# Neighbourhood attention at the two edge blocks of the grid: 384 keys per query tile in place of 512

## The chip, the cores and the metric

The kernel runs on one core of one Trainium2 chip. The metric is the device time of one launch in microseconds. A core has five engines with a queue of instructions each: TensorE (PE in the profile; its weight loads have a row of their own, PEld), VectorE (DVE), ScalarE (ACT), GpSimd (POOL) and SyncE (SP), which here issues every DMA.

## The reference, cut to what matters

One encoder layer over 2048 tokens of width 1024. A combined projection gives six pieces; the first two go through a state-space model (S5), the other four through neighbourhood attention on a grid of 32 rows by 64 columns, and both results are projected out and mixed with the residual. The part that the change touches:

```python
def neighborhood_attention_2d(q, k, v, rpb):
    rows = seqlen // GRID_W            # 32 rows of 64 tokens
    kh = min(NA_ROWS_MAX, rows)        # 8
    row_start = jnp.clip(r - kh // 2, 0, rows - kh)
    col_start = jnp.clip(c - NA_COLS // 2, 0, GRID_W - NA_COLS)   # 16 columns
    ...
    scores = jnp.einsum('brqhd,brikhd->bhrqik', q, k_blk) * scale + bias
    scores = jnp.where(col_in[:, None, :], scores, jnp.finfo(f32).min)
    probs = jax.nn.softmax(scores, axis=(-2, -1))
    out = jnp.einsum('bhrqik,brikhd->brqhd', probs, v_blk)
```

Each of 8 heads of 64 dimensions lets a query see 8 rows by 16 columns of neighbours. The window is clamped at the grid's borders, so queries of the uppermost 8 rows reach no key below row 10, and queries of the lowest 8 rows none above row 20.

## The kernel before, in words

The kernel has three stages: a projection and state-space stage (to about 650 us of the span), attention beside other matmuls (about 655 to 1056 us), and a dense last stage (to 1387 us).

**Units and steps.** Attention runs over 16 units. A unit is one pair of heads (`hp`, the pair lies in partitions 0 to 63 and 64 to 127) and one block `i` of 8 grid rows. The first eight units are blocks 1 and 2, the last eight are the edge blocks 3 and 0 (`na_units`, L681). A unit has four steps, one for each query tile `j` of 8 rows by 16 columns, 128 queries; so there are 64 steps, and steps 32 to 63 belong to edge blocks. For every tile the keys are a frame of 16 rows by 32 columns, 512 keys, that starts 4 rows above the block. In an edge block four of these rows lie outside the grid; there the frame holds rows of the other edge, and the bias (-1e30) masks them.

**One step**, for each head of the pair:
- `scores` (L718): a matmul of 64 rows by 128 columns of weights with 512 moving columns into PSUM tile `p_qk` (L726; two tiles, one for each head, in all). DVE adds the bias and takes the row minimum (L730), ACT takes the exponential and its sum (L732), DVE the reciprocal (L733), POOL the product (L734).
- `turn` (L738): four transposes of 128 by 128 into `p_pt` (L744), one ACT copy to SBUF (L746).
- `weigh` (L749): the product with v for one group `jk` of key columns that two query tiles share: two matmuls a head of 256 moving columns (L757), for the lower and upper half of the 16 rows. The two heads' matmuls write partitions 0 to 63 and 64 to 127 of the PSUM tile `po`.

All operands are fp32; of each L726 and L757 matmul the trace has two records (two passes), of each transpose one.

**What sets the order.** `attention` (L760) writes two steps a round: turn, scores, products of two earlier steps, turn, scores, and then `fill`, a counted number of matmuls of other work (`beside`, L872): the last projections, the GLU (L662), and from about 876 us on the output projection of eight mix tiles (`mix_tile`, L855, matmuls L834). PE's order is fixed by the program (`issue_after`). The orders of the other queues, SP's too, and of the instructions inside one `scores` call are made by the framework's scheduler from its own model of time.

**Loads.** Each unit's bias (L697), q (L699), k (L702), v (L703) and gate zn (L705) come by DMA from DRAM into rings of two buffers, and a load waits until the unit before last has let its buffer go. The result of a unit goes out at L713 (`yn_scr`); a mix tile loads it back at L860, casts it on ACT (L863, `yh`), takes the rest on DVE (L864, `yl`), and its two PSUM banks are copied out by ACT (L868) and DVE (L869). Three banks serve these tiles, so the second matmul of a tile waits for a copy of the tile before.

Of the kernel before, what the change touches and what calls it, by code (L numbers as in the profile page):

```python
# [50 lines left out]
class Layer:  # L51
# [633 lines left out]
    def na_units(self):  # L685
# [4 lines left out]
        for blocks in ((1, 2), (3, 0)):  # L690
            for hp in range(4):
                kind = None
                for n, i in enumerate(blocks):
                    it = (0, 1, 1, 2)[i]
                    if it != kind:
                        bm, kind = self.b_bm(), it
                        nc.sync.dma_start(bm, a["bias"][hp, it])  # L697
                    q, k, v, zn = self.b_q(), self.b_k(), self.b_v(), self.b_zn()
                    nc.sync.dma_start(q, self.q_scr[hp][:, 512 * i : 512 * i + 512])  # L699
                    for lo, rows in ((0, slice(i - 1, i + 1)),) if i else ((0, slice(3, 4)), (1, slice(0, 1))):  # L700
                        c = slice(512 * rows.start, 512 * rows.stop)
# [13 lines left out]

                    yield js, q, k, v, bm, done

    def scores(self, j, q, k, bm):  # L718

        nc, c = self.nc, self.const  # L720
        ps, out = [self.ps2("qk") for _ in range(2)], []
        for par in range(2):
            own = slice(64 * par, 64 * par + 64)
            kk = k[own]
            mv = ap_of(kk, max(16 * (j - 1), 0), [list(kk.ap[0]), [48 if j == 0 else 16, 2], [64, 16], [1, 16]])
            nc.tensor.matmul(ps[par], q[own, 128 * j : 128 * j + 128], mv, start=True, stop=True)  # L726
        for par in range(2):
            s = self.b_s()
# [9 lines left out]
    def turn(self, j, ss, pts):  # L738

        nc = self.nc  # L740
        for s, pT in zip(ss, pts):
            pt = self.ps2("pt")
            for n in range(4):
                nc.tensor.transpose(pt[:, 128 * n : 128 * n + 128], s[:, 128 * n : 128 * n + 128], self.ident)  # L744
            base, step = ((j - 1) * 512 + 128, 512 if j == 3 else 384) if j else (0, 1536)
            nc.scalar.copy(ap_of(pT, base, [list(pT.ap[0]), [step, 2], [256, 2], [1, 128]]),  # L746
                           pt.rearrange("p (j i q) -> p j i q", j=2, i=2))

    def weigh(self, po, jk, v, pts, first, last):  # L749

        for rb in range(2):
            for par in range(2):
                own = slice(64 * par, 64 * par + 64)
                pw = po[own]
                o = ap_of(pw, 128 * jk % 384, [list(pw.ap[0]), [384 if jk == 3 else 128, 2], [1, 128]])
                c = 512 * jk + 256 * rb
                self.nc.tensor.matmul(o, v[:, 4 * rb + jk, own], pts[par][:, c : c + 256],  # L757
                                      start=first and rb == 0, stop=last and rb == 1, skip_group_check=True)

    def attention(self, fill):  # L760
# [9 lines left out]
        def turn(t):  # L770
            if 0 <= t < STEPS:
                _, j, ss, pp = st[t]
                run(self.turn, j, ss, pp)

        def score(t):
            if t < STEPS:
# [4 lines left out]
                with self.tc.issue_after(self.last_pe()):  # L781
                    st[t] = (u, j, self.scores(j, u[1], u[2], u[4]), pts)

        def product(t):
            if 0 <= t < STEPS:
                n = t % 4
                (_, _, _, v, _, done), j, _, pp = st.pop(t)
                if n == 0:
                    self.po = self.ps.tile([128, 512], F32, tag="pv", name="po", bufs=1)
                else:  # L790
                    run(self.weigh, self.po, (j - 1) % 4, v, pp, n == 1, False)
                if n == 3:
                    run(self.weigh, self.po, j, v, pp, False, True)
                    done(self.po)
# [195 lines left out]
def biases(rpb):  # L990
# [3 lines left out]
    for it, i in enumerate((0, 1, 3)):  # L994
        for jt, j in enumerate((0, 1, 3)):
            qr, qc = (8 * i + np.arange(128) // 16)[:, None], (16 * j + np.arange(128) % 16)[:, None]
            r0, c0 = np.clip(qr - 4, 0, 24), np.clip(qc - 8, 0, 48)
            n = np.arange(512)
            half, rr, cc = n // 256, n // 16 % 16, n % 16
            kr = (8 * i - 4 + rr)[None, :]  # L1000
# [49 lines left out]
```

## Time and profile before

| what | value |
|---|---|
| median of 3 runs | 1385.05 us (1382.8 to 1385.6) |
| the profiled execution | 1388.96 us, span of its trace 1387.2 us |
| PE busy over the span | 1319.9 us (95%) |
| DVE, ACT, POOL busy | 895.0 us (65%), 461.0 us (33%), 560.2 us (40%) |
| edge blocks, 841 to 1056 us | PE busy 201.9 of 215 us, clock 0.88 to 1.00 |

Busy time is the union of an engine's instructions. Matmuls are pipelined: a record lasts longer than the distance to the next one, so the time that PE needs for a row of matmuls is read from where the next group starts. The granted clock is TensorE's, 1.00 being 2.4 GHz and 0.50 being 1.2 GHz.

### The profile page before, as it was taken

The numbers are of one execution on the slowest core, as the hardware profiler recorded it, in microseconds if no ns is written. First come the engines' busy times: TensorE is split into PE (matmuls) and PEld (weight loads), VectorE is DVE, ScalarE is ACT, GpSimd is POOL, SyncE is SP. The second block draws the span as 40 slices with busy tenths as digits, with TensorE's granted clock in tenths as the row PEclk, the third lists the DMA queues.
The fourth block names the chain that finished last, engine by engine and source line by source line (L and its number), as shares of the span: only waits on it lengthen the run. The fifth ranks groups of instructions, "written<-read, shape, count | busy, mean of one in ns | idle before, by whom it ended". The sixth has DMA issues, their size and how long they took to land. (4 is left out here: it accounts for less than half of the span.)

```text
span 1387.2 us, 19010 instructions
## 1 busy us (share of the span) xinstructions
PE 1319.9 (95%) x6432; PEld 1026.2 (74%) x6432; DVE 895.0 (65%) x1851; ACT 461.0 (33%) x957; POOL 560.2 (40%) x695
## 2 busy tenths in 40 slices
PE   7897999999999999999996898999999999999998
PEld 6675778888878888887664676666667888888887
DVE  5864899888977779533456566533343344888886
ACT  7520211111111122112555565644443322333322
POOL 5968789677766665000333444222220000121121
PEclk9998999999999999999998999999999999999999
DMA  8873223223333332226357567746425532333331
GB/s 280 247 204 84 75 86 100 86 85 97 91 82 80 84 82 90 80 74 217 114 173 258 185 216 241 254 161 226 152 77 193 179 106 83 100 121 119 106 123 63
DMA packets 177665, 190.01 MB, mean 137 GB/s; under 512 B 46496, under 2 KB 136992, under 8 KB 175904
## 3 DMA queue, kind: packets, MB, share of 16 engines
q1 hardware_dynamic: 177568, 188.80, 43.3%
q8 instruction: 51, 0.84, 0.2%
q14 instruction: 46, 0.38, 0.1%
HBM read 131.44 MB, written 57.31 MB: 136 GB/s over the span
## 5 line engine op out<-in xcount | busy, mean ns | idle before, releaser
L205 PE MATMUL pd<-xh,wh 128*128 128x512 f32 x768 | 311.6, 407 | 19.5 <-DVE ev_u L267 12.4
L205 PE MATMUL pd<-xl,wh 128*128 128x512 f32 x768 | 308.2, 402 | 0.0
L205 PE MATMUL pd<-xh,wl 128*128 128x512 f32 x768 | 307.7, 401 | 0.0
L734 POOL TENSOR_SCALAR na<-na,rs 128x512 f32<-128x512 f32 x128 | 94.8, 744 | 365.4 <-DVE rs L733 304.2
L205 PEld LDWEIGHTS pd<-xh,wh 128*128 128x128 f32 x768 | 146.0, 190 | 57.8 <-DVE ev_u L267 13.5
L205 PEld LDWEIGHTS pd<-xh,wl 128*128 128x128 f32 x768 | 145.7, 190 | 38.7 <-issue 4.0
L205 PEld LDWEIGHTS pd<-xl,wh 128*128 128x128 f32 x768 | 145.9, 190 | 35.7 <-issue 1.5
L730 DVE CUSTOM_DVE_ANT_0 na<-p_qk,na 128x512 f32<-128x512 f32 x128 | 83.8, 687 | 115.9 <-PE p_qk L726 112.1
L977 POOL TENSOR_TENSOR p3e<-p3e,p 128x1024 f32<-128x1024 f32 x15 | 39.2, 2611 | 292.7 <-DVE p3e L972 284.9
L834 PE MATMUL pd<-wo,yh 128*128 128x512 f32 x512 | 142.5, 394 | 7.3 <-ACT o L868 4.1
L834 PE MATMUL pd<-wg,yh 128*128 128x512 f32 x512 | 140.7, 391 | 0.0
L834 PEld LDWEIGHTS pd<-wo,yh 128*128 128x128 f32 x512 | 96.0, 189 | 34.7 <-ACT o L868 5.4
L732 ACT ACTIVATE na<-na,mn 128x512 f32<-128x512 f32 x128 | 91.7, 717 | 66.9 <-DVE mn L730 66.5
L834 PEld LDWEIGHTS pd<-wg,yh 128*128 128x128 f32 x512 | 95.5, 188 | 19.2
L746 ACT COPY na<-p_pt 128x512 f32<-128x512 f32 x128 | 68.8, 583 | 76.3 <-PE p_pt L744 76.3
L178 ACT ACTIVATE wh<-wr 128x512 fp32r<-128x512 f32 x48 | 28.1, 624 | 164.1 <-PE pd L205 146.8
L834 PE MATMUL pd<-wo,yl 128*128 128x512 f32 x256 | 81.8, 394 | 0.0
L834 PE MATMUL pd<-wg,yl 128*128 128x512 f32 x256 | 81.3, 391 | 0.0
L744 PE MATMUL p_pt<-ident,na 128*128 128x128 f32 x512 | 70.9, 282 | 8.7 <-POOL na L734 6.4
L726 PE MATMUL p_qk<-na,na 64*128 64x512 f32 x256 | 76.5, 653 | 2.5 <-DVE mn L730 2.5
L744 PEld LDWEIGHTS p_pt<-ident,na 128*128 128x128 f32 x512 | 58.6, 144 | 25.1 <-issue 13.7
L757 PE MATMUL po<-na,na 128*64 128x256 f32 x512 | 63.2, 390 | 0.0
(203 smaller groups left out, 2256.5 us busy)
## 6 DMA issues: line engine op xcount, KB each, us to landing
na<-in_bias_dram SPq DMA_DIRECT2D x12, 1536.0 KB
wr<-in_w_in_dram SPq DMA_DIRECT2D x48, 256.0 KB
xr<-in_xT_dram SPq DMA_DIRECT2D x32, 256.0 KB
xn<-in_x_dram SPq DMA_DIRECT2D x32, 256.0 KB
o_scr<-o SPq DMA_DIRECT2D x16, 512.0 KB
p<-o_scr SPq DMA_DIRECT2D x16, 512.0 KB
xt<-in_x_dram SPq DMA_DIRECT2D x16, 512.0 KB
out_dram<-p3e SPq DMA_DIRECT2D x15, 512.0 KB
```

The source lines that it names most:

```text
L178: nc.scalar.mul(wh[:, sl], wr, mul)
L205: nc.tensor.matmul(ps, st[:, k, :], mv[:, k, :], start=n == 0, stop=n == 3 * KT - 1)
L726: nc.tensor.matmul(ps[par], q[own, 128 * j : 128 * j + 128], mv, start=True, stop=True)
L730: nc.vector.tensor_tensor_reduce(out=s, in0=ps[par], in1=bm[:, par, (0, 1, 1, 2)[j]], scale=-1.0, scalar=3e38, op0=ALU.add, op1=ALU.min, a ...
L732: nc.scalar.activation(s, s, AF.Exp, bias=mn, scale=-1.0, accum_out=sm)
L734: nc.gpsimd.tensor_scalar(s, s, rs, 1.0, ALU.mult, ALU.mult)
L744: nc.tensor.transpose(pt[:, 128 * n : 128 * n + 128], s[:, 128 * n : 128 * n + 128], self.ident)
L746: nc.scalar.copy(ap_of(pT, base, [list(pT.ap[0]), [step, 2], [256, 2], [1, 128]]), pt.rearrange("p (j i q) -> p j i q", j=2, i=2))
L757: self.nc.tensor.matmul(o, v[:, 4 * rb + jk, own], pts[par][:, c : c + 256], start=first and rb == 0, stop=last and rb == 1, skip_group_ch ...
L834: nc.tensor.matmul(ps[e], st[:, k, :], mv[k][:, 512 * e : 512 * e + 512], start=k == 0 and n == 0, stop=k == nk - 1 and n == 2)
L977: nc.gpsimd.tensor_add(th, th, h1)
```

## The change

For the eight units of blocks 3 and 0 the frame of keys is cut to the 12 rows that lie in the grid, 8 rows first (`kt` = 0 or 1 says which half of the frame they are) and then 4: 384 keys. Units of blocks 1 and 2 keep 512 (`kt` is None). The scores of a head become a matmul of 256 and one of 128 columns; the minimum, exponential and product run over 384 columns; three transposes in place of four; and the product with v becomes, for each `jk`, one matmul a head of 256 columns over the 8-row half (L779), and for each tile `j` one a head of 128 columns over the 4 rows (new `weigh_rest`, L786), for which 64 partitions hold rows of one column half and 64 of the other. The bias load brings 384 of 512 columns (still two heads by three tiles), so each partition's piece becomes six pieces. The v load of an edge unit becomes five DMAs (one of 256 KB, two of 96 KB, two of 32 KB) in place of one of 512 KB (block 3) or two of 256 KB (block 0). For all units the transposed probabilities are stored in one row for each tile, and the product reads two stretches of 128 columns in place of one of 256.

```diff
@@ na_units
+                    kt = (1, None, None, 0)[i]
                     if it != kind:
                         bm, kind = self.b_bm(), it
-                        nc.sync.dma_start(bm, a["bias"][hp, it])
+                        nk = 512 if it == 1 else 384
+                        nc.sync.dma_start(bm[:, :, :, 0:nk], a["bias"][hp, it][:, :, :, 0:nk])
...
-                        nc.sync.dma_start(v[:, 4 * lo : 4 * lo + 4 * (rows.stop - rows.start)],
-                                          self.v_scr[hp][rows].rearrange("i j p d -> p (i j) d"))
+                    if it == 1:
+                        nc.sync.dma_start(v, self.v_scr[hp][i - 1 : i + 1].rearrange("i j p d -> p (i j) d"))
+                    else:
+
+                        nc.sync.dma_start(v[:, 4 * kt : 4 * kt + 4], self.v_scr[hp][0 if i == 0 else 2].rearrange("j p d -> p j d"))
+                        vl = v[:, 4 - 4 * kt : 8 - 4 * kt]
+                        rest = self.v_scr[hp][3][:, 64 * kt : 64 * kt + 64].rearrange("j p d -> p j d")
+                        nc.sync.dma_start(vl[0:64, 1:4], rest[:, 0:3])
+                        nc.sync.dma_start(vl[64:128, 1:4], rest[:, 1:4])
+                        nc.sync.dma_start(vl[0:64, 0:1], rest[:, 0:1])
+                        nc.sync.dma_start(vl[64:128, 0:1], rest[:, 3:4])
@@ scores
+        n, rows = (512, ((0, 16),)) if kt is None else (384, ((8 * kt, 8), (8 - 4 * kt, 4)))
+        at = 0
+        for r0, nr in rows:
+            for par in range(2):
+                own = slice(64 * par, 64 * par + 64)
+                kk = k[own]
+                mv = ap_of(kk, max(16 * (j - 1), 0) + 64 * r0,
+                           [list(kk.ap[0]), [48 if j == 0 else 16, 2], [64, nr], [1, 16]])
+                nc.tensor.matmul(ps[par][:, at : at + 32 * nr], q[own, 128 * j : 128 * j + 128], mv, start=True, stop=True)
+            at += 32 * nr
...
-            nc.vector.tensor_tensor_reduce(out=s, in0=ps[par], in1=bm[:, par, (0, 1, 1, 2)[j]], scale=-1.0, scalar=3e38,
-                                           op0=ALU.add, op1=ALU.min, accum_out=mn)
+            nc.vector.tensor_tensor_reduce(out=s, in0=ps[par][:, 0:n], in1=bm[:, par, (0, 1, 1, 2)[j], 0:n], scale=-1.0,
+                                           scalar=3e38, op0=ALU.add, op1=ALU.min, accum_out=mn)
@@ turn
-            for n in range(4):
-                nc.tensor.transpose(pt[:, 128 * n : 128 * n + 128], s[:, 128 * n : 128 * n + 128], self.ident)
+            n = 512 if kt is None else 384
+            for x in range(0, n, 128):
+                nc.tensor.transpose(pt[:, x : x + 128], s[:, x : x + 128], self.ident)
+            nc.scalar.copy(pT[:, n * j : n * j + n], pt[:, 0:n])
@@ weigh
+        n, wide = (512, 2) if kt is None else (384, 1)
+        at = lambda q, h: n * q + 128 * wide * h
+        for rb in range(wide):
...
+    def weigh_rest(self, po, j, v, pts, kt):
+
+        for par in range(2):
+            own = slice(64 * par, 64 * par + 64)
+            self.nc.tensor.matmul(po[own, 128 * j : 128 * j + 128], v[:, 4 - 4 * kt + j, own],
+                                  pts[par][:, 384 * j + 256 : 384 * j + 384], start=False, stop=False, skip_group_check=True)
@@ attention, product
+                    if kt is not None:
+                        for jj in js[0 if n == 1 else n : n + 1]:
+                            run(self.weigh_rest, self.po, jj, v, pp, kt)
```

PE, one round in the edge blocks, before: transposes (`p_pt`), scores (`p_qk`), product with v (`po`), transposes, scores; the row's end says how many matmuls run one after another.

```order
L744 MATMUL p_pt<-ident,na_5624 128x128 x8
L726 MATMUL p_qk<-na_5623,na_5621 128x512 x2
L757 MATMUL po<-na_5626,na_5623 64x256 x4
L744 MATMUL p_pt<-ident,na_5624 128x128 x8
L726 MATMUL p_qk<-na_5623,na_5621 128x512 x2
```

The corresponding round of the changed kernel, after the same matmuls of the mix tile:

```order
L763 MATMUL p_pt<-ident,na_5624 128x128 x6
L742 MATMUL p_qk<-na_5623,na_5621 128x256 x2
L742 MATMUL p_qk<-na_5623,na_5621 128x128 x2
L779 MATMUL po<-na_5626,na_5623 64x256 x2
L786 MATMUL po<-na_5626,na_5623 64x128 x4
L763 MATMUL p_pt<-ident,na_5624 128x128 x6
L742 MATMUL p_qk<-na_5623,na_5621 128x256
L742 MATMUL p_qk<-na_5623,na_5621 128x128
L742 MATMUL p_qk<-na_5623,na_5621 128x256
L742 MATMUL p_qk<-na_5623,na_5621 128x128
```

Two transposes of eight are gone in each step, and the first scores stand as 256, 256, 128, 128 columns (heads 0, 1, 0, 1). In the second scores of the round the scheduler has put both matmuls of head 0 ahead of those of head 1. The fill between rounds has the same number of matmuls as before in every round.

SP's queue, before, where the loads of the second edge unit meet the first mix tile's load (`y<-yn_scr_122`):

```order
L671 DMA ys_scr_120<-zs 128x1024
L642 DMA zs<-zs_scr_95 128x1024
L703 DMA na_5623<-v_scr_87 128x8x128
L713 DMA yn_scr_122<-na_5622 128x512
L705 DMA na_5624<-zn_scr_94 128x512
L699 DMA na_5621<-q_scr_79 128x512
L702 DMA na_5623<-kk_scr_83 128x512
L697 DMA na_5622<-in_bias_dram 128x3072
L702 DMA na_5623<-kk_scr_83 128x512
L860 DMA y<-yn_scr_122 128x4x128
```

The same place after:

```order
L714 DMA na_5623<-v_scr_87 64x128
L709 DMA na_5623<-v_scr_87 128x4x128
L712 DMA na_5623<-v_scr_87 64x3x128
L724 DMA yn_scr_122<-na_5622 128x512
L713 DMA na_5623<-v_scr_87 64x3x128
L715 DMA na_5623<-v_scr_87 64x128
L716 DMA na_5624<-zn_scr_94 128x512
L701 DMA na_5621<-q_scr_79 128x512
L699 DMA na_5622<-in_bias_dram 128x6x384
L704 DMA na_5623<-kk_scr_83 128x512 x2
L892 DMA y<-yn_scr_122 128x4x128
L671 DMA ys_scr_120<-zs 128x1024
```

The store of `yn_scr_122` now stands behind three of the five pieces of v, and two further pieces, in all four more issues, stand ahead of the mix tile's load; the bias load has 384 of 512 columns.

## Rows read from the trace of the kernel before

**Rows 1.** The page, busy time of each engine over the span.

```profile
PE 1319.9 (95%) x6432; PEld 1026.2 (74%) x6432; DVE 895.0 (65%) x1851; ACT 461.0 (33%) x957; POOL 560.2 (40%) x695
```

**Rows 2.** Windows: stretch, length, busy time by engine, granted clock, DMA share, GB/s.

```profile
841.00:870.00 29.00, 25.32 (x152) 18.00 (x151) 16.59 (x37) 15.98 (x35) 12.27 (x13) 0.88 0.73 249
870.00:1041.00 171.00, 163.67 (x900) 110.00 (x899) 67.19 (x196) 84.89 (x188) 39.27 (x56) 1.00 0.51 172
1041.00:1056.00 15.00, 12.88 (x72) 9.87 (x72) 3.17 (x4) 4.81 (x8) 0.02 (x1) 0.89 0.41 133
1056.00:1387.00 331.00, 325.84 (x1505) 270.18 (x1501) 225.22 (x595) 99.04 (x208) 39.16 (x15) 1.00 0.36 119
```

**Rows 3.** PE's waits in 841-870, then 870-1041: us, times, longest.

```profile
PE pd L662 <- ACT th L667: 1.8, 1, 1.8
PE p_qk L726 <- DVE mn L730: 1.8, 2, 1.1
...
PE pd L834 <- ACT o L868: 4.1, 3, 1.4
PE pd L834 <- DVE o L869: 3.2, 3, 1.3
```

**Rows 4.** Timeline of PE: start, length, instructions, number of records; edge rounds.

```profile
942.40 1.03 PE L744 MATMUL p_pt<-ident,na 128*128 128x128 f32 x8
943.36 1.13 PE L726 MATMUL p_qk<-na,na 64*128 64x512 f32 x4
944.42 1.08 PE L757 MATMUL po<-na,na 128*64 128x256 f32 x8
...
956.39 2.81 PE L757 MATMUL po<-na,na 128*64 128x256 f32 x24
```

**Rows 5.** The same timeline cut at 943.6 us: scores begun by then.

```profile
943.36 0.70 PE L726 MATMUL p_qk<-na,na 64*128 64x512 f32 x2
```

**Rows 6.** Timeline of PE in the stage before: one matmul of 256 columns.

```profile
577.77 0.59 PE L568 MATMUL p_qk<-x,gt 128*128 128x256 f32 x2
```

**Rows 7.** Groups by line on PE, 841-1056 us: records, busy us, mean ns, idle.

```profile
L726 PE MATMUL p_qk<-na,na 64*128 64x512 f32 x128 | 38.0, 646 | 1.8 <-DVE mn L730 1.8
L744 PE MATMUL p_pt<-ident,na 128*128 128x128 f32 x268 | 36.8, 280 | 2.2 <-ACT na L746 2.1
L757 PE MATMUL po<-na,na 128*64 128x256 f32 x284 | 34.6, 385 | 0.0
```

**Rows 8.** Instructions of lines L730, L732, L667: ns min/median/max, first and last start.

```profile
L730 DVE CUSTOM_DVE_ANT_0 na<-p_qk,na x128: 672/687/693, 656.8 to 1036.9; 128x512 f32<-128x512 f32 x128
...
L732 ACT ACTIVATE na<-na,mn x128: 704/722/727, 657.5 to 1038.8; 128x512 f32<-128x512 f32 x128
...
L667 ACT ACTIVATE th<-pd,bgh x32: 451/460/478, 744.0 to 877.1; 128x256 f32<-128x256 f32 x32
```

**Rows 9.** Timeline of SP and ACT around the first mix tile's load.

```profile
834.21 0.37 SPq L703 DMA_DIRECT2D na<-v_scr  x1
834.93 0.33 SPq L713 DMA_DIRECT2D yn_scr<-na  x1
...
837.73 0.33 SPq L697 DMA_DIRECT2D na<-in_bias_dram  x1
...
841.22 0.57 SPq L860 DMA_DIRECT2D y<-yn_scr  x1
...
849.73 1.05 ACT L863 CAST yh<-y 128x1024 fp32r<-128x1024 f32 x1 [3.66 <-DMA y<-yn_scr]
```

**Rows 10.** Windows, columns as in group 2: the slow stretch behind these waits.

```profile
861.60:868.20 6.60, 6.60 (x27) 5.47 (x26) 4.12 (x12) 4.87 (x12) 2.71 (x4) 0.50 0.95 286
```

**Rows 11.** Timeline of SP: loads of a later edge unit.

```profile
909.99 0.93 SPq L703 DMA_DIRECT2D na<-v_scr  x2
...
913.94 0.33 SPq L697 DMA_DIRECT2D na<-in_bias_dram  x1
```

More of the change, by code (lines that the diff above doesn't have):

```diff
@@ L714, in done, with scores @@
                         self.attended += n
-                    yield js, q, k, v, bm, done
-    def scores(self, j, q, k, bm):
+                    yield js, q, k, v, bm, done, kt
+    def scores(self, j, q, k, bm, kt):
         nc, c = self.nc, self.const
         ps, out = [self.ps2("qk") for _ in range(2)], []
-        for par in range(2):
[L723 to L728, printed above, removed]
+        n, rows = (512, ((0, 16),)) if kt is None else (384, ((8 * kt, 8), (8 - 4 * kt, 4)))
[8 more added lines that the diff above has]
+            at += 32 * nr
+        for par in range(2):
+            s = self.b_s()[:, 0:n]
             mn, sm, rs = (c.tile([128, 1], F32, tag=t, name=t, bufs=8) for t in ("mn", "sm", "rs"))
-            nc.vector.tensor_tensor_reduce(out=s, in0=ps[par], in1=bm[:, par, (0, 1, 1, 2)[j]], scale=-1.0, scalar=3e38,
-                                           op0=ALU.add, op1=ALU.min, accum_out=mn)
+            nc.vector.tensor_tensor_reduce(out=s, in0=ps[par][:, 0:n], in1=bm[:, par, (0, 1, 1, 2)[j], 0:n], scale=-1.0,
+                                           scalar=3e38, op0=ALU.add, op1=ALU.min, accum_out=mn)
             nc.scalar.activation(s, s, AF.Exp, bias=mn, scale=-1.0, accum_out=sm)
@@ L742, in turn, with weigh @@
             pt = self.ps2("pt")
-            for n in range(4):
-                nc.tensor.transpose(pt[:, 128 * n : 128 * n + 128], s[:, 128 * n : 128 * n + 128], self.ident)
[L745 to L751, printed above, removed]
+            n = 512 if kt is None else 384
+            for x in range(0, n, 128):
+                nc.tensor.transpose(pt[:, x : x + 128], s[:, x : x + 128], self.ident)
+            nc.scalar.copy(pT[:, n * j : n * j + n], pt[:, 0:n])
+    def weigh(self, po, jk, v, pts, kt, first, last):
+        (qa, ha), (qb, hb) = ((0, 1), (3, 1)) if jk == 3 else ((jk, int(jk > 0)), (jk + 1, 0))
+        n, wide = (512, 2) if kt is None else (384, 1)
+        at = lambda q, h: n * q + 128 * wide * h
+        for rb in range(wide):
             for par in range(2):
@@ L754, in weigh @@
                 pw = po[own]
[L755 to L758, printed above, removed]
+                o = ap_of(pw, 128 * qa, [list(pw.ap[0]), [128 * (qb - qa), 2], [1, 128]])
+                pT = pts[par]
+                mv = ap_of(pT, at(qa, ha) + 128 * rb, [list(pT.ap[0]), [at(qb, hb) - at(qa, ha), 2], [1, 128]])
+                self.nc.tensor.matmul(o, v[:, 4 * (rb if kt is None else kt) + jk, own], mv,
+                                      start=first and rb == 0, stop=last and rb == wide - 1, skip_group_check=True)
+    def weigh_rest(self, po, j, v, pts, kt):
[3 more added lines that the diff above has]
+                                  pts[par][:, 384 * j + 256 : 384 * j + 384], start=False, stop=False, skip_group_check=True)
     def attention(self, fill):
@@ L771, in turn @@
             if 0 <= t < STEPS:
-                _, j, ss, pp = st[t]
-                run(self.turn, j, ss, pp)
+                u, j, ss, pp = st[t]
+                run(self.turn, j, ss, pp, u[6])
         def score(t):
@@ L781, in score @@
                 with self.tc.issue_after(self.last_pe()):
-                    st[t] = (u, j, self.scores(j, u[1], u[2], u[4]), pts)
+                    st[t] = (u, j, self.scores(j, u[1], u[2], u[4], u[6]), pts)
         def product(t):
@@ L997, in biases @@
             r0, c0 = np.clip(qr - 4, 0, 24), np.clip(qc - 8, 0, 48)
-            n = np.arange(512)
-            half, rr, cc = n // 256, n // 16 % 16, n % 16
+            r = np.concatenate([np.stack(np.meshgrid(np.arange(2), x, np.arange(16), indexing="ij"), -1).reshape(-1, 3)
+                                for x in ((np.arange(8, 16), np.arange(4, 8)), (np.arange(16),),
+                                          (np.arange(8), np.arange(8, 12)))[it]])
+            half, rr, cc = r.T
             kr = (8 * i - 4 + rr)[None, :]
```

8 lines of the change are left out of this document (4 added, 4 removed).

## The prediction

> **What bounds the kernel now.** I read the page first: PE is busy for 95% of the span [rows 1], no other engine for more than 65%. An average over stages says little, so the windows come next. In the edge blocks' stretch, 841 to 1056 us, PE is busy 25.3 + 163.7 + 12.9 of 215 us; in its long middle it is busy for 163.7 of 171 us at clock 1.00, while DVE has 67 and ACT 85 of the 171 us, and in the dense last stage PE has 325.8 of 331 us [rows 2]. What PE waits for there is short: 7.3 us in the middle, all of it for the copies of a mix tile's PSUM banks, and 3.6 us at the start of the stretch [rows 3]. PE's order and its fill are the same before and after, so PE time taken out of the edge steps moves everything behind it forward. The sum is therefore one of PE time; the other engines' savings count only where PE waits for them.
>
> **What PE pays for a column.** Durations don't tell, since records overlap; distances do. A product group of 24 records lasts 2.81 us and one of 8 lasts 1.08 [rows 4]: 16 more records, 1.73 us. The records run in pairs, as the scores show: two of them are under way by 943.6, together 0.70 us long, though one alone has a mean of 646 ns, and all four end after 1.13 us [rows 4, 5, 7]. A pair must be the two heads, since the two passes of one matmul use the same rows of weights. So 1.73 us are 8 pair-passes of 256 columns, 0.216 us each. A lone matmul of 256 columns, two records in 0.59 us with a last one of about 0.38, is paced at 0.21 a pass as well [rows 6], the 0.38 being the mean of the same width among the products [rows 7]: two heads cost what one does. By that a pass of 512 columns takes 0.432 us, and the scores, which begin at 943.36 and give way at 944.42, are 2 x 0.432 plus 0.20 for the two changes of array layout [rows 4].
>
> **The change, part by part.**
> - Transposes. Eight take 1.03 us [rows 4], the last of them 0.28 [rows 7], so they stand (1.03 - 0.28) / 7 = 0.107 us apart. Two fewer in each of 32 steps: 64 x 0.107 = 6.9 us.
> - Scores. Two passes of 512 columns become two of 256 and two of 128. No row has fp32 products of 128 columns. The price lies between 0.108 us, half of 256 columns, and 0.216, were 256 a floor. The nearest row is the transposes: 128 columns of fp32 with a 128-column weight load each, 0.107 apart, so loading q's weights twice is hidden at that pace; I take 0.108. A step saves 2 x (0.432 - 0.216 - 0.108) = 0.216 us, 32 steps 6.9 us. Changes of layout stay as many.
> - Product. A unit has 16 pair-passes of 256 columns; it gets 8 of 256 and 8 of 128 (four `jk`, four tiles, two passes each). 16 x 0.216 - 8 x 0.216 - 8 x 0.108 = 0.86 us, eight units 6.9 us. That the moving operand is now two stretches of 128, also in the first half, costs nothing: the scores already read theirs in pieces of 16 and keep the 0.432.
> - DVE, ACT, POOL. The minimum takes 687 ns for 512 columns, so 384 take 515 (in proportion) to 687. ACT needs 722 for 512 and 460 for 256 columns [rows 8], so about 590 for 384. These engines have spare time; where PE waits for a bank copy the minimum and the exponential stand before it, about 0.3 us less a wait, six waits. Against that, in two of them the scheduler has put a reciprocal that needs the exponential ahead of DVE's copy, about 0.3 us more. I enter 0, bounds -2 and +1 us.
> - DMA. The bias load shrinks by a quarter; v comes in five pieces, 28 more issues, each about 0.4 us of SP [rows 9]. The cover is the ring of two: the v load issued at 909.99 is first used by the products at 944.42, the bias load of 913.94 behind the scores at 943.36 [rows 4, 11], 34 and 29 us. If that cover were gone, a late load would stop PE directly. I enter 0.
>
> Sum: 6.9 + 6.9 + 6.9 = 20.7 us. The profiled execution took 1388.96 us (span 1387.2), so it would take 1368.3; it lies 3.9 us above the median of the runs, and from the median the forecast is 1385.05 - 20.7 = **1364.3 us**. As a bound from above, a quarter of the three lines' busy time, (38.0 + 36.8 + 34.6) / 4 = 27.4 us [rows 7], which counts the layout changes and tails too, as if they shrank.
>
> **The rivals.**
> - *The heads no longer pair in the second scores of a round.* There both matmuls of head 0 now stand ahead of head 1's. Pairing needs head 1 to overtake. In the trace it overtakes one pass: a matmul is two passes, the second head's first starts with the first head's first [rows 5], though head 0's second stands ahead of it. Now it would have to overtake three. If it can't, only the last pass of 128 overlaps: 0.648 + 0.648 - 0.108 = 1.19 us in place of 0.648, 0.54 us in 16 rounds, 8.6 us lost: 1364.3 + 8.6 = 1373 us. For it: no row shows an overtaking by three. Against it: the two heads run in step through 24 records on end. The Trainium skill, "TensorE: Matmul & The Clock Gate", section "The mechanism", says that matmuls never leave program order and only weight loads are pulled ahead. By that rule the rival would hold; this trace's pairs already go against the rule as worded, so I give it less than even odds.
> - *128 columns cost what 256 do.* The 64 + 64 pair-passes of 128 columns then cost 0.108 us more each, 13.8 us: 1378 us. Transposes of 128 columns at 0.107 speak against it.
> - *The start of the stretch heals.* ACT's cast stands waiting for the first mix tile's load (issued 841.22, cast 849.73) [rows 9], everything on ACT stands behind it, PE waits 1.8 + 1.8 us [rows 3], and then the clock is at 0.50 for some 6.8 us, of which 6.6 are shown [rows 10], half of that lost: about 7 us in all. A smaller bias load in front of that load, and a scheduler order that puts the second head's minimum ahead of the `yl` that waits, could take out part: 1358 to 1361.
> - *Slower.* The same place the other way. The store of `yn` stands behind three pieces of v and the mix tile's load behind four more issues, about 1.6 us of SP; until the cast, ACT holds two steps' softmax and PE runs dry at once. Each us that the load lands later is a us of PE, and a longer half clock costs half its length more. To be slower than 1385 it must lose 20.7 us: the load would have to land some 14 to 20 us later than 849.7, some three times its present 8.5 us. Only the 1.6 us is in sight, and 384 KB less bias against it. The Trainium skill, "DMA: Bandwidth & Descriptors", section "Rules for kernel authors", advises against splitting a transfer by halves of partitions, and against pieces under 64 KB, both of which the v load now does; no row here shows such a piece. 1386 to 1392 us.
> - *No change:* the saving goes into PE's bank waits, because the copies, not PE, set them. They would have to grow from 7.3 to 28 us while the work ahead of them shrinks.
>
> **How the numbers follow.** Forecast, 1361 to 1368: 0.63. Unpaired heads, 1369 to 1374: 0.14. A floor at 256 columns or another loss that leaves a gain, 1374 to 1382: 0.07. A healed start, 1357 to 1361: 0.11. No change (within 0.2%, 2.8 us, about what a measurement of this kernel can tell from none): 0.02. Slower: 0.03. Faster is 0.95. The range from 1359 to 1374 holds the forecast, the unpaired heads and about half of the healed start, 0.82; the ends are not stretched to the floor of 256 columns.
>
> **What the next profile would show.** Transposes six in about 0.82 us; first scores giving way to the product 0.85 us after their start; the second scores as long as the first (paired), or about 1.4 us (not); a product group of three `jk` and two tiles in about 1.95 us in place of 2.81. PE's busy time about 20 us less, its waits in the middle still 6 to 8 us, the mix tile's cast within 2 us of 849.7. I am wrong if the 128-column passes stand further apart than 0.12 us, if a wait for `v_scr`, `kk_scr` or bias appears on PE or DVE, or if the clock falls between 870 and 1041 us.

## The result, and the profile after

The changed kernel took 1368.8 us (median of 20 runs), the kernel before 1385.3 (20 runs); the ratio is 0.989, with a 95% interval from 0.9867 to 0.9912. By the ratio that is 15.2 us less (12 to 18; the medians differ by 16.5). The whole interval lies below 1, so the change is faster. The time lies inside the range of 1359 to 1374, 4.5 us above the forecast of 1364.3 and 0.8 above the band of 1361 to 1368 that went with it. The profiled execution took 1369.4 us, its span is 1367.0.

PE's busy time, to be read beside [rows 1], is 20.1 us less:

```profile
PE 1299.8 (95%) x6496; PEld 1031.5 (75%) x6496; DVE 884.5 (65%) x1851; ACT 447.0 (33%) x957; POOL 554.1 (41%) x695
```

The windows of after answer to [rows 2] and [rows 10]; the columns are the same. The cuts are the first edge scores, the first mix matmul, a place behind the last scores, and the end of the last product.

```profile
837.00:873.00 36.00, 28.51 (x204) 23.20 (x203) 18.18 (x48) 17.61 (x44) 12.44 (x15) 0.83 0.77 241
873.00:1021.00 148.00, 141.13 (x910) 109.75 (x910) 56.00 (x185) 69.48 (x180) 31.14 (x54) 1.00 0.53 167
1021.00:1037.00 16.00, 13.27 (x77) 9.99 (x76) 3.20 (x5) 4.33 (x9) 0.37 (x1) 0.89 0.47 152
1037.00:1367.00 330.00, 324.88 (x1497) 270.08 (x1497) 225.62 (x595) 99.27 (x208) 39.11 (x15) 1.00 0.36 119
...
847.20:854.00 6.80, 5.02 (x23) 3.85 (x25) 3.47 (x5) 4.53 (x12) 4.21 (x4) 0.50 0.51 154
867.60:874.40 6.80, 5.76 (x25) 4.98 (x26) 3.90 (x14) 4.97 (x15) 2.00 (x4) 0.50 0.92 328
```

In the middle PE is still dense at clock 1.00, and the last stage is as it was. The start is worse than before: granted clock 0.83 over 36 us, because the clock now falls to 0.50 twice, from 847.2 and from 867.6 us, each time within one of PE's two long waits of the start (they end at 848.98 and 868.64); before it fell there once [rows 10]. PE's waits (us, times, longest), first of 825 to 890 us, then of 890 to 1050, beside [rows 3]:

```profile
PE pd L662 <- ACT th L667: 3.8, 1, 3.8
PE p_pt L763 <- ACT na L764: 3.7, 1, 3.7
...
PE pd L866 <- DVE o L901: 3.5, 3, 1.2
PE pd L866 <- ACT o L900: 3.4, 3, 1.1
PE p_pt L763 <- ACT na L764: 2.7, 1, 2.7
```

The middle has 6.9 us of bank waits for 7.3 before. The start has 7.5 for 3.6, in two pieces of almost 4 us.

Where the time came from is read by steps, from the start of the scores of steps 32 (the first edge step), 40 and 62 on PE's timeline, of after and of before:

```profile
837.05 0.49 PE L742 MATMUL p_qk<-na,na 64*128 64x256 f32 x2
...
890.16 0.49 PE L742 MATMUL p_qk<-na,na 64*128 64x256 f32 x2
...
1012.49 0.49 PE L742 MATMUL p_qk<-na,na 64*128 64x256 f32 x2
...
1036.31 0.60 PE L779 MATMUL po<-na,na 128*64 128x256 f32 x4
```

```profile
841.32 0.70 PE L726 MATMUL p_qk<-na,na 64*128 64x512 f32 x2
...
894.04 0.70 PE L726 MATMUL p_qk<-na,na 64*128 64x512 f32 x2
...
1030.18 0.70 PE L726 MATMUL p_qk<-na,na 64*128 64x512 f32 x2
...
1055.69 1.03 PE L757 MATMUL po<-na,na 128*64 128x256 f32 x8
```

From step 32 to the end of the last product it is 199.9 us after (1036.91 - 837.05) and 215.4 before: 15.5 us saved, about what the ratio says. The profiled spans differ by 20.2; of the rest 4.3 lie ahead of step 32. The first attention step comes 3.4 us earlier (655.6 us before, 652.2 after), and the change touches nothing ahead of it. Steps 0 to 31, where only the layout of the transposed probabilities changed, took 0.9 us less (185.7 before, 184.9 after; 182.8 to 186.0 in e1, e2 and e9). Both are taken for a difference between executions. The 15.5 divide unevenly. From step 40 on, 24 of the 32 steps, 162.7 became 146.75: 15.9 us, where 24/32 of the forecast's 20.7 is 15.5. In the first eight steps 52.7 became 53.1, where 8/32 of 20.7, 5.2 us, should have gone. All that is missing, 5.6 us, is missing there.

### The profile page after: what moved, and what is told of

Read it like the earlier page. It is cut to its first block, busy times and chain, and to the rows that moved or that the text cites. A ratio compares the mean times of both kernels' runs of the same rounds, so it can differ in the third digit from the quotient of the medians.

```text
span 1367.0 us, 19180 instructions
## 1 busy us (share of the span) xinstructions
PE 1299.8 (95%) x6496; PEld 1031.5 (75%) x6496; DVE 884.5 (65%) x1851; ACT 447.0 (33%) x957; POOL 554.1 (41%) x695
## 4 chain that ended last, share of the span: by engine, by line
PE 76%; DVE 8%; DMA 7%; POOL 4%; issue 3%; ACT 2%; SPq 1%; DVEq 0%; ACTq 0%; POOLq 0%
PE pd L205 30%; PE pd L866 24%; PE p_qk L742 4%; PE p_qk L866 3%; PE p_pt L763 3%; PE po L779 3%; PE p_pt L535 2%; DMA raw<-in_w_out_dram 2%; PE pd L662 2%; DMA ys_scr<-zs 1%; PE p_pt L983 1%; DMA xn<-in_x_dram 1%; PE p_qk L568 1%; DMA wr<-in_w_in_dram 1%; DVE ev_u L267 1%
## 5 line engine op out<-in xcount | busy, mean ns | idle before, releaser
L751 POOL TENSOR_SCALAR na<-na,rs 128x512 f32<-128x512 f32 (+1 forms) x128 | 88.3, 693 | 356.5 <-DVE rs L750 276.4
L205 PEld LDWEIGHTS pd<-xh,wh 128*128 128x128 f32 x768 | 145.5, 189 | 53.1 <-DVE ev_u L267 8.9
L747 DVE CUSTOM_DVE_ANT_0 na<-p_qk,na 128x512 f32<-128x512 f32 (+1 forms) x128 | 75.2, 621 | 107.8 <-PE p_qk L742 105.5
L749 ACT ACTIVATE na<-na,mn 128x512 f32<-128x512 f32 (+1 forms) x128 | 84.8, 663 | 59.2 <-DVE mn L747 57.9
L764 ACT COPY na<-p_pt 128x512 f32<-128x512 f32 (+1 forms) x128 | 61.7, 529 | 71.7 <-PE p_pt L763 71.6
L763 PE MATMUL p_pt<-ident,na 128*128 128x128 f32 x448 | 64.3, 284 | 12.2 <-ACT na L764 6.4
L763 PEld LDWEIGHTS p_pt<-ident,na 128*128 128x128 f32 x448 | 51.9, 145 | 27.0 <-issue 16.4
L742 PE MATMUL p_qk<-na,na 64*128 64x512 f32 (+2 forms) x384 | 69.8, 461 | 0.8 <-DVE mn L747 0.8
L280 ACT ACTIVATE ev_th<-ev_z 128x512 f32<-128x512 f32 x32 | 20.1, 629 | 111.2 <-DVE ev_z L278 98.8
```

The lines of the kernel that those rows point to most:

```text
L205: nc.tensor.matmul(ps, st[:, k, :], mv[:, k, :], start=n == 0, stop=n == 3 * KT - 1)
L742: nc.tensor.matmul(ps[par][:, at : at + 32 * nr], q[own, 128 * j : 128 * j + 128], mv, start=True, stop=True)
L747: nc.vector.tensor_tensor_reduce(out=s, in0=ps[par][:, 0:n], in1=bm[:, par, (0, 1, 1, 2)[j], 0:n], scale=-1.0, scalar=3e38, op0=ALU.add, o ...
L763: nc.tensor.transpose(pt[:, x : x + 128], s[:, x : x + 128], self.ident)
L764: nc.scalar.copy(pT[:, n * j : n * j + n], pt[:, 0:n])
```

## The experiments

Three theories for the missing 5 us were tried. **A**: the pieces in which v is now loaded delay the loads that stand behind them, of the first mix tile's `y` and of `w_out`; ACT, which works in order, stands at the casts that wait for them, and PE runs dry. **B**: PE only comes to the same place earlier, and the loads take what they took. **C**: the pieces do nothing, but the scheduler chose another order of ACT's instructions with them. A fourth, **D**, has no run of its own: the transfers of the pieces do nothing, but the scheduler chose another order of SP's issues with them. The two queues of SP ahead of the prediction show it: before, the bias load stands between the two k loads, after, ahead of both. The links from load to PE, on SP and ACT of after:

```profile
837.08 0.68 SPq L892 DMA_DIRECT2D y<-yn_scr  x1
...
856.46 0.36 SPq L843 DMA_DIRECT2D raw<-in_w_out_dram  x1
...
859.98 0.43 SPq L843 DMA_DIRECT2D raw<-in_w_out_dram  x1
...
846.32 1.04 ACT L895 CAST yh<-y 128x1024 fp32r<-128x1024 f32 x1 [5.14 <-DMA y<-yn_scr]
...
867.14 0.62 ACT L844 CAST wo<-raw 128x512 fp32r<-128x512 f32 x1 [4.72 <-DMA raw<-in_w_out_dram]
867.66 0.47 ACT L667 ACTIVATE th<-pd,bgh 128x256 f32<-128x256 f32 x1
868.03 0.85 ACT L764 COPY na<-p_pt 128x384 f32<-128x384 f32 x2
```

The cast of `yh` stood 5.1 us for a load issued 9.2 us earlier (8.5 before [rows 9]), and the `th` for which PE waits came behind it; the cast of `wo` stood 4.7 us, and the copies of `p_pt` that PE waits for came behind that one. Its load took 7.2 us (859.98 to 867.14) and was issued 3.5 us behind the `w_out` load ahead of it, with three pieces of v between the two on SP. Before, the two stand together, and the second of them, issued 0.6 us behind the first, took 3.7 us:

```profile
859.87 0.94 SPq L811 DMA_DIRECT2D raw<-in_w_out_dram  x2
...
864.18 0.62 ACT L812 CAST wo<-raw 128x512 fp32r<-128x512 f32 x1
```

This table holds, for the profiled execution of each kernel, the us from step 32 to 40, from 40 to 62, and from 32 to the end of the last product, the us from the issue of the first mix tile's `yn` load to its cast, the half-clock stretches of the first eight steps (us), and the median time with the ratio to the kernel before on the same chip:

```
                       32-40  40-62  32-end  y load  half clock   median   ratio (95%)
before                  52.7  136.1  215.4    8.5    6.8          1385.3
after                   53.1  122.3  199.9    9.2    6.8 + 6.8    1368.8   0.9890 (0.9867-0.9912)
e1 v in two loads       47.0  122.3  193.6    7.1    none         1365.3   0.9874 (0.9846-0.9902)
e2 before, five pieces  57.4  136.1  218.7    9.8    3.4 + 6.8    1386.8   1.0045 (1.0006-1.0084)
e3 cast of yh later     49.7  122.3  196.3    8.9    6.8          1368.7   0.9885 (0.9856-0.9914)
e4 third raw buffer     48.2  122.3  193.2    8.7    3.4          1367.7   0.9898 (0.9860-0.9935)
e5 four full pieces     46.3  122.3  192.9    7.0    none         1362.4   0.9847 (0.9797-0.9897)
e6 two halves           46.4  122.3  193.3    6.6    none         1365.7   0.9844 (0.9803-0.9886)
e7 v put together       46.2  122.3  193.1    6.4    none         1365.2   0.9851 (0.9812-0.9890)
e9 as e1, after's order 47.1  122.4  194.5    7.5    none         1365.4   0.9861 (0.9814-0.9909)
e12 32 KB joined        48.2  122.3  194.8    6.8    6.8          1363.9   0.9827 (0.9786-0.9869)
e8 scores 256 + 256     51.8  126.8  203.0    9.4    3.4          1384.5   one run
e10 four transposes     50.9  126.9  200.6    9.2    6.8          1371.4   one run
e11 products 256        52.9  127.0  205.1    8.9    6.8 + 6.8    1372.2   one run
```

The times of e1 to e12 come from four chips and their intervals are 0.6 to 1.0% wide, so the steps, which don't hold the stages ahead, tell more than the medians. The six kernels of the change without the two 32 KB pieces of v (e1, e5, e6, e7, e9, e12) all have a lower ratio than the change, 0.983 to 0.987, though each interval overlaps with the change's.

**e1: v in two loads.**

```
-  nc.sync.dma_start(vl[0:64, 1:4], rest[:, 0:3])
-  nc.sync.dma_start(vl[64:128, 1:4], rest[:, 1:4])
-  nc.sync.dma_start(vl[0:64, 0:1], rest[:, 0:1])
-  nc.sync.dma_start(vl[64:128, 0:1], rest[:, 3:4])
+  nc.sync.dma_start(vl, self.v_scr[hp][3].rearrange("j p d -> p j d"))
```

> The changed kernel, with the 64 + 64 key rows of v for the edge units in one load of a whole tile in place of four pieces: the same bytes, 24 issues fewer. Every value of the second key tile then belongs to another key, so the output differs; all else is the same work. Theory A (the four pieces hold SP's queue and the transfers behind them, and that is what cost about 5 us at the start of the edge stretch): PE's waits between 830 and 885 us fall from 7.5 back to about 3.6, one half-clock stretch in place of two, and 1364 us (0.985 of the kernel before). Theory B (PE comes 5 us earlier to the same loads of the first mix tile and of w_out, which take as long as ever, and ACT hands their lateness on): waits of 6 to 8 us, two half-clock stretches, 1369 us (0.988 to 0.989).

The first eight steps took 47.0 us, the clock did not fall there, and PE's waits were 5.4 us (A asked for one fall and 3.6). This is what the forecast's sum asks for (52.7 - 5.2 = 47.5). B falls, since the load of `y` took 7.1 us and not as long as ever. C and D are left, since the orders of ACT and SP differ from those of after.

**e2: the five pieces in the kernel before.** The same four lines and the first tile's load, put into the kernel before.

> The kernel before, with only its v loads of the edge units replaced by the five pieces of the change; 512 keys are computed as before (the second half of them from another arrangement of v, so the output differs). Theory A: the start of the stretch loses 4 to 5 us, 1390 us (1.003 to 1.004). Theory B: no loss, 1385 us (0.999 to 1.001), PE's waits there about 3.6 us as before.

The first eight steps took 4.7 us longer, the time is 0.45% above that of before. The two waits of after are there, with 512 keys:

```profile
PE pd L662 <- ACT th L667: 4.1, 1, 4.1
PE p_pt L753 <- ACT na L755: 3.1, 1, 3.1
```

So the loss comes with the pieces and not with fewer columns or a PE that comes early. The orders of ACT and SP changed with them here too, so C and D stay. Up to the last product 3.3 of the 4.7 us are left, because in this execution the clock did not fall in the last steps, as it does before from 1045.8 us.

**e3: the cast of `yh` queued later on ACT.**

```
...
-        nc.scalar.copy(yh, y)
+        with self.tc.issue_after(self.ths[-5] if t == 4 else self.ths[0]):
+            nc.scalar.copy(yh, y)
```

> The changed kernel, with ACT's cast of the first mix tile's y queued behind the tanh of the third quarter-set of the last gate block, so that the copies, exponentials and tanhs that PE needs no longer stand behind a cast that waits for its load. Nothing is left out. If ACT's order carries the first wait to PE (A and B alike): the 3.8 us wait for th goes, with it the half-clock stretch after it (3.4 us), unless the second wait grows by as much: 1362 to 1366 us. If PE waits for the load itself: the wait only changes its name, 1369 us.

The wait for `th` went, but another took its place:

```profile
PE p_qk L747 <- DVE mn L752: 5.7, 1, 5.7
```

The minimum stood on DVE behind two `zs` of the GLU and behind `yl`. What came late was not the cast that `yl` needs (849.29 to 850.34) but `zs`: DVE waited for POOL, and POOL for another load.

```profile
854.04 1.52 POOL L660 TENSOR_TENSOR zs<-zs,glu_x 128x512 f32<-128x512 f32 x1 [6.17 <-DMA zs<-zs_scr]
...
855.59 2.44 DVE L674 SCALAR_TENSOR_TENSOR zs<-th,zs 128x256 f32<-128x256 f32 x2 [8.09 <-POOL zs L660]
857.95 1.21 DVE L902 TENSOR_TENSOR yl<-y,yh 128x1024 fp32r<-128x1024 f32 x1
```

The steps gained 3.4 us in the profiled execution, the median nothing that can be told; the 1362 to 1366 us were missed. That ACT's order handed the first load's lateness to PE is shown by the wait that went. As a cure it is half of one, because a second late load, of `zs`, then stops PE by way of POOL and DVE.

**e4: a third buffer for the raw pieces of `w_out`.**

```
+  self.nr = getattr(self, "nr", -1) + 1
-  r = self.rp.tile([128, 512], F32, tag="raw", name="raw", bufs=2)
+  r = (self.mp.tile([128, 512], F32, tag="rw", name="raw", bufs=1) if self.nr % 3 == 2 else
+       self.rp.tile([128, 512], F32, tag="raw", name="raw", bufs=2))
```

> The changed kernel, with three buffers in place of two for the raw pieces of w_out, so that the third and later loads are issued without waiting for a cast. Nothing is left out. If the third load was late because it was issued late, behind v and the bias (B, and A in part): the second wait of 3.7 us goes with its half-clock stretch (3.4 us), 1362 to 1365 us. If the transfers themselves are saturated there (A: by the pieces of v): the load lands when it did, 1369 us.

The second wait shrank from 3.7 to 0.8 us and the steps took 48.2, but the first load was late still (8.7 us), and the median, 1367.7, is not to be told from that of the change. ACT's order changed as well. e8 and e10 below, which leave the loads as they are in after, bear on the same wait: there the scheduler put the second `w_out` load 0.6 and 1.6 us behind the one ahead of it (3.5 in after), it took 2.8 and 3.9 us (7.2), and PE waited for the copies 0.8 and 2.3 us (3.7). So the second wait goes with the place of that load on SP.

**e5 and e6: other pieces.** One edit each in place of e1's added line: four loads of one slot on 128 partitions, and two loads of four slots on 64.

```
+  for s in range(4):
+      nc.sync.dma_start(vl[:, s : s + 1], self.v_scr[hp][3][s : s + 1].rearrange("j p d -> p j d"))
```

```
+  nc.sync.dma_start(vl[0:64], rest)
+  nc.sync.dma_start(vl[64:128], rest)
```

> The changed kernel with the second key tile of v in four loads again, but each of one slot over all 128 partitions (64 KB) in place of halves of 64 partitions: five issues a unit as in the change, the same bytes, other keys in that tile, so the output differs. If the number of issues and their small size is what delays the loads behind them: the eight steps from step 32 take 52 to 53 us as in the change, 1369 us. If it is that each piece fills only half of the partitions: about 47 us as with two loads, 1365 us.

> The changed kernel with the second key tile of v in two loads of 64 partitions each with all four slots (128 KB): three issues a unit; other keys in that tile, so the output differs. PE, ACT and DVE have the same order of instructions as in the run with two loads. If halves of the partitions are the cost: 50 to 53 us for the eight steps from step 32 and 1367 to 1369 us. If the number of issues is: near the run with two loads, 47 to 48 us and 1365 us.

Both took 46.3 to 46.4 us for the eight steps, and the load of `y` 6.6 to 7.0. Five issues a unit cost nothing by themselves, and neither do halves of the partitions. In both, as in e1, the bias load stands between the k loads on SP.

**e7: a version that loads v whole.** Where v is written, the lower tile of the edge units is put together in DRAM once, so that an edge unit loads it in one piece.

```
...
+  e = self.ve_scr[m][int(to != b)].rearrange("j p d -> p j d")
+  nc.sync.dma_start(e[0:64, 1:4], src[:, 0:3])
+  nc.sync.dma_start(e[64:128, 1:4], src[:, 1:4])
+  nc.sync.dma_start(e[0:64, 0:1], src[:, 0:1])
+  nc.sync.dma_start(e[64:128, 0:1], src[:, 3:4])
...
+  nc.sync.dma_start(v[:, 4 - 4 * kt : 8 - 4 * kt], self.ve_scr[hp][kt].rearrange("j p d -> p j d"))
```

> The changed kernel, with the second key tile of the edge units put together where v is written, in the dense stage (eight stores of 32 and 96 KB per pair of heads in place of two of 128 KB), so that an edge unit loads it in one piece. Nothing is left out. If the pieces of v cost the 5 us at the start of the edge stretch and the dense stage hides the extra stores: 1364 us (0.984 to 0.986), about 47 us for the eight steps from step 32. If the stores are not hidden there: the time before the first attention step grows from 652 us, and the gain is gone.

The steps are those of e1 (193.1 us from step 32 to the end, 22.3 less than before), the median is 1365.2, the ratio 0.9851. The profiled execution reached its first attention step at 663.9 us (652.2 after), but those of e4 and e8, which store nothing more, reached theirs at 667, so whether the added stores are hidden is not settled; five of six timed runs lie between 1360.9 and 1366.9. By its ratio it is the best of the kernels here that leave nothing out; its interval overlaps with that of the change.

**e9: loads of e1, order of after.** Five casts are held behind the ACT instructions that they follow in after (`issue_after`, as in e3), which makes PE's, ACT's and DVE's orders those of after row for row.

> The run with two loads of v (e1) again, its other keys in the second tile included, with five casts on ACT held back so that PE, ACT and DVE have exactly the order of instructions of the changed kernel; only the loads, and SP's order of them, differ from it. Theory A (the way in which v's pieces are transferred delays the loads behind them): about 47 us for the eight steps from step 32, no or one short half-clock stretch, 1365 us. Theory C (the pieces do nothing by themselves; the other order of ACT that the scheduler chose with them costs the 5 us): 52 to 53 us, both half-clock stretches, 1369 us.

47.1 us, no fall of the clock, waits of 5.0. C falls. What is left between e9 and after is the loads of v and SP's order: A or D. Of the 6.0 us between the two (53.1 - 47.1) PE's waits account for 2.5 (7.5 and 5.0); the other 3.5 go with the two half-clock stretches, of which e9 has none. In e9, issue and cast of the load, PE's waits, and two windows: the whole start, and the stretch from the load's issue to its cast.

```profile
844.73 0.53 SPq L897 DMA_DIRECT2D y<-yn_scr  x1
...
852.26 1.05 ACT L901 CAST yh<-y 128x1024 fp32r<-128x1024 f32 x1 [3.04 <-DMA y<-yn_scr]
```

```profile
PE p_pt L765 <- ACT na L766: 1.7, 1, 1.7
PE pd L666 <- ACT th L671: 1.6, 1, 1.6
PE p_qk L744 <- DVE mn L749: 1.4, 2, 1.2
PE p_pt L765 <- POOL na L753: 0.3, 1, 0.3
```

```profile
844.00:885.00 41.00, 35.97 (x279) 29.03 (x278) 24.70 (x60) 23.33 (x58) 15.26 (x18) 1.00 0.78 258
...
844.73:852.26 7.53, 7.17 (x59) 5.84 (x59) 3.98 (x11) 3.00 (x9) 4.07 (x5) 1.00 0.99 348
```

The same window of after, from issue to cast:

```profile
837.08:846.32 9.24, 8.13 (x66) 6.70 (x65) 3.60 (x12) 2.98 (x9) 3.59 (x5) 1.00 0.86 275
```

The last two columns are the point: the same load, with about as many bytes moved meanwhile (rate times length, 2.5 and 2.6 MB), with the 16 DMA engines busy for 0.86 of the time at 275 GB/s with the pieces, and for 0.99 at 348 without. (A transfer is counted where it starts, so a short window can come out above 1.) The difference is largest right behind the issue; the first 1.5 us of after, then of e9:

```profile
837.08:838.58 1.50, 1.50 (x15) 1.15 (x16) 1.50 (x3) 0.72 (x2) 1.50 (x2) 1.00 0.69 173
...
844.73:846.23 1.50, 1.50 (x15) 1.17 (x16) 1.50 (x1) 0.74 (x2) 1.50 (x2) 1.00 1.02 353
```

**e12: which pieces.** Only the two smallest, 64 partitions by one slot, joined into one of 128 partitions; those of 96 KB stay.

```
-  nc.sync.dma_start(vl[0:64, 0:1], rest[:, 0:1])
-  nc.sync.dma_start(vl[64:128, 0:1], rest[:, 3:4])
+  nc.sync.dma_start(vl[:, 0:1], self.v_scr[hp][3][0:1].rearrange("j p d -> p j d"))
```

> The changed kernel with only its two smallest pieces of v (64 partitions, one slot, 32 KB each) joined into one of 128 partitions (64 KB); the two of 96 KB on 64 partitions stay. Four issues a unit; the slot's keys differ, so the output does. If the 32 KB pieces are what delays the loads behind them: the load of the first mix tile's y takes 6.4 to 7.5 us from issue to cast, as in the runs that lost nothing, and the eight steps from step 32 take 46 to 48 us. If it is the 96 KB pieces of three slots on half of the partitions: 8.7 to 9.8 us for the load and 50 to 53 us for the eight steps.

```profile
836.33:843.08 6.75, 6.66 (x55) 5.35 (x55) 3.76 (x12) 2.49 (x8) 3.76 (x5) 1.00 1.02 359
```

The load took 6.8 us and the steps 48.2 (46 to 48 expected): with the two pieces of 32 KB joined, 4.9 of the 6.0 us between after and e9 are gone. But SP's order changed with them:

```profile
832.90 0.44 SPq L704 DMA_DIRECT2D na<-kk_scr  x1
833.44 0.59 SPq L699 DMA_DIRECT2D na<-in_bias_dram  x1
834.26 0.45 SPq L704 DMA_DIRECT2D na<-kk_scr  x1
```

The bias load stands between the k loads again, as it does in e1, e5, e6, e7 and e9, whose load of `y` took 6.4 to 7.5 us, and in the kernel before (8.5 us, with 384 KB more of bias). In all seven executions with the 32 KB pieces (after, e2, e3, e4, e8, e10, e11), where the load took 8.7 to 9.8 us, it stands ahead of both. So e12 does not tell the transfers of the small pieces (A) from the order that comes with them (D). The clock still fell once, for 6.8 us, with no wait of PE over 1.9 us, while e1 had one of 2.1 and no fall; so the last 1 us is not settled by one execution.

**e8, e10, e11: the three terms of the sum.** Each gives PE one part of its old work back.

```
e8   -  ((8 * kt, 8), (8 - 4 * kt, 4))
e8   +  ((8 * kt, 8), (8 - 8 * kt, 8))
e10  +  if n == 384:
e10  +      nc.tensor.transpose(pt[:, 384:512], s[:, 256:384], self.ident)
e11  -  self.nc.tensor.matmul(po[own, 128 * j : 128 * j + 128], ..., pts[par][:, 384 * j + 256 : 384 * j + 384], ...)
e11  +  self.nc.tensor.matmul(po[own, c : c + 256], ..., pts[par][:, 384 * j + 128 : 384 * j + 384], ...)
```

> The changed kernel, with the scores' second matmul 256 columns wide again in place of 128; DVE, ACT and the rest still work on 384, so only TensorE's passes come back and the output stays the same. By the prediction's sum (0.108 us for each of 64 pair-passes, 6.9 us; 24 of 32 steps lie behind step 40): the stretch from step 40 to the last product grows from 146.75 us by 5.2 to 151.9. If 128 columns cost what 256 do: no change there.

> The changed kernel with a fourth transpose of each head in the edge steps, into columns that nobody reads: eight a step as before, and nothing left out. By the prediction's 0.107 us each, 48 of them behind step 40: the stretch from step 40 to the last product grows from 146.75 us by 5.1 to 151.9; if the transposes were hidden, it stays.

> The changed kernel with the product's 128-column matmuls made 256 columns wide again (the second half goes to columns of other queries, so the output differs): 64 pair-passes of 256 in place of 128. By the prediction's 0.108 us each, 48 of them behind step 40: the stretch from step 40 to the last product grows from 146.75 us by 5.2 to 151.9; with a floor at 256 columns it stays.

In e8 the 128 columns kept are those of other keys at both edges, so that, other than its expectation says, the output changes; the widths are as said. From step 40 to the last product the three took 151.3, 149.75 and 152.2 us. e10 falls short of its 151.9 mostly because in its execution the clock did not fall in the last steps, where that of after does for 3.4 us from 1028.1. From 40 to 62, free of that, they added 4.4, 4.5 and 4.7 us; 22/32 of 6.9 is 4.7. Together 13.6, of 13.8 us that the change saves there.

## Why the prediction came near, and what it missed

**The sum held.** Each price came out as told: in an edge round of after, to be read beside [rows 4],

```profile
922.98 0.81 PE L763 MATMUL p_pt<-ident,na 128*128 128x128 f32 x6
923.73 0.92 PE L742 MATMUL p_qk<-na,na 64*128 64x256 f32 x8
924.58 0.65 PE L779 MATMUL po<-na,na 128*64 128x256 f32 x4
925.06 0.39 PE L786 MATMUL po<-na,na 128*64 128x128 f32 x4
925.28 0.60 PE L779 MATMUL po<-na,na 128*64 128x256 f32 x4
925.71 0.39 PE L786 MATMUL po<-na,na 128*64 128x128 f32 x4
925.93 0.60 PE L779 MATMUL po<-na,na 128*64 128x256 f32 x4
...
927.27 0.93 PE L742 MATMUL p_qk<-na,na 64*128 64x256 f32 x8
```

six transposes take 0.81 us (0.82 told), the first scores give way after 0.85 (0.85), the product group runs from 924.58 to 926.53 (1.95). Two pair-passes of 128 columns take 0.22 us (925.06 to 925.28), 0.11 each, where more than 0.12 was the sign of being wrong. e8, e10 and e11 show that each term is within 0.3 us of its forecast over 22 steps.

**Unpaired heads** did not come: the second scores last 0.93 us like the first, and not 1.4. **A floor at 256 columns** did not come either (e8, e11: widening 128 to 256 costs what the sum says). DVE and ACT behaved as told; the mean of 384 columns is 554 ns for the minimum (515 to 687 told) and 610 for the exponential (590):

```profile
L749 ACT ACTIVATE na<-na,mn 128x384 f32<-128x384 f32 x64 | 39.0, 610 | 27.8 <-DVE mn L747 26.7 <-POOL na L751 1.1
...
L747 DVE CUSTOM_DVE_ANT_0 na<-p_qk,na 128x384 f32<-128x384 f32 x64 | 33.3, 554 | 71.4 <-PE p_qk L742 71.4
```

**The step that failed** is the DMA term, "If that cover were gone, a late load would stop PE directly. I enter 0". The cover was worked out for v and the bias, and for these it held: no wait for them shows on PE or DVE. But the loads that pay are those behind them, which ACT comes to wait for 2 to 4 us after their issue, and not 29 or 34. The rival "slower" had the place and the links right (late load, cast, ACT, PE, clock) and the size wrong: it counted 1.6 us of SP's issues. The load of `y` is issued with the first edge scores as before (837.08 and 837.05, before 841.22 and 841.32) and loses its time between issue and cast: 9.2 us for 8.5 before and 7.5 without the pieces (e9). A second load, of `w_out`, which the prediction did not look at, took 7.2 us for 3.7 before. Together 6.0 us, after against e9.

**The start did not heal** either. Without the pieces the eight steps took 46.2 to 47.1 us (e1, e5, e6, e7, e9), 0.4 to 1.3 less than the sum's 47.5, where the rival asked for 3 to 6. The load came earlier and the half-clock stretch went, but PE's waits were 4.2 to 5.4 us there, for 3.6 before.

**The signs.** The sign "the cast within 2 us of 849.7" failed (846.32) and was of little use, as the stretch began 4.3 us earlier; the time from issue to cast is the one to look at. The sign "if the clock falls between 870 and 1041 us" came by the letter: it was at 0.50 until 874.4 us, the end of the start's second stretch, and for 3.4 us from 1028.1, which is the fall of the last steps, from 1045.8 us before, moved ahead with them.

**What was luck.** The band of the forecast itself ended at 1368. That the range held 1368.8 is owed to the 1369 to 1374 beside it, which were there for unpaired heads: another cause that did not come would have given nearly the same time.

The Trainium skill, "TensorE: Matmul & The Clock Gate", section "The mechanism", has matmuls stay in program order. The scores of 927.27, where both matmuls of one head stand first, show the two heads in step for 0.93 us, so the trace does not agree for two heads in different rows of the array. The Trainium skill, "DMA: Bandwidth & Descriptors", section "Rules for kernel authors", says that under 64 KB one pays mostly overhead and advises one transfer over two on halves of the partitions. e12 is in keeping with the first at 32 KB, though SP's order changed with it, and e6 shows no price for halves of 128 KB.

**Open** is by what the change slows the loads behind v: by the transfers of the two pieces of 32 KB (A) or by the order of SP that came with them in every run (D). The loads of e9 in the order of after, or those of after with the bias held between the k loads, would tell. Shown is that the DMA engines are idle meanwhile, 0.86 busy against 0.99 to 1.02, and most of all right behind the issue. That the bias load is issued late is not enough by itself: in e5 it stands 2.0 us ahead of the load of `y`, in after 2.4, and e5 loses nothing; but e5 has a k load ahead of it. The records don't say which engine moved what, so an uneven spread over the engines is only a guess.

## What to carry to other kernels

Price work on the bound engine by the distance between records, and the saving will be found where that engine stays dense. For a load that the change splits, ask not only whether its own user is covered but which loads stand behind it in the queue, whether the split moves them there, and who waits for those in order; look at their time from issue to use. Where a reordered layout can be put together once at the writer, the reader's load can stay in one piece (e7).

## What the runs showed of the hardware that was not expected

With two loads of 32 KB each, on 64 partitions, and the order of SP that came with them, a 256 KB load issued 4 and 7 us after them took 9.2 us (after) in place of 6.8 (e12), and the rate was 275 GB/s in place of 359. Four loads of 64 KB on 128 partitions, without that order, did no such thing (e5, 7.0 us). Which of the two does it is not shown.

In the second scores of a round the program has both matmuls of head 0, of 256 and 128 columns, ahead of those of head 1. Their records start in pairs all the same, four of 256 columns and then four of 128, and the eight take 0.93 us, as in the first scores (0.92).
